# Rolling the rows of an 8192 x 8192 matrix by 100 columns: two rows in one flat copy of 65024 B instead of one row per copy

## The chip, the core and the metric

The kernel runs on one core of a Trainium2 chip. A core has compute engines (TensorE, VectorE, ScalarE, GpSimd), a SyncE that only issues work, and 16 DMA engines which move data between the chip's large memory (HBM, here called DRAM as well) and the on-chip memory SBUF, or from HBM to HBM. DMAs are issued by an instruction of SyncE (SP in the profile), ScalarE (ACT) or GpSimd (POOL). Each of the three has its own queue on every DMA engine. The metric is the device time of one execution in microseconds; lower is better.

## The reference

The kernel computes a roll along the columns: every element moves 100 columns to the right, and what leaves on the right comes back on the left of the same row.

```python
x = np.random.randn(8192, 8192).astype(np.float32)   # shift = 100
def reference(x, shift):
    return np.roll(x, shift, axis=1)     # out[r, c] = x[r, (c - 100) mod 8192]
```

Nothing is calculated. 256 MiB (268.44 MB) are read and as many written, and the work is in where the bytes go.

## The kernel before

In the code `s` is 100, `a` is 128 (the shift rounded up to 128 columns, so that a piece begins at a multiple of 512 B in the output) and `g` is 28. Each output row of 32768 B has two parts.

**The bulk**, columns 128 to 8191 (8064 elements, 32256 B), is one contiguous piece of the input row, at column 28. It is copied from DRAM to DRAM without touching SBUF. The rows are taken in 128 blocks of 64. Within a block, DMA `j` (0 to 3) takes the 16 rows `4e + j`, one for each DMA engine `e`; `j` = 0 and 2 are issued by SP, 1 and 3 by ACT (L41). So each DMA holds 16 pieces of 32256 B whose starts lie 128 KB apart. In the last four blocks a row is cut in two (15872 and 16384 B), two DMAs per `j`.

**The head**, columns 0 to 127 (512 B), consists of the row's last 100 input columns and its first 28. It goes through SBUF, on GpSimd's queue, in 16 stages of 512 rows (128 partitions x 4 rows). For rows 0 to 2 of a partition one DMA (L70) reads the 128 contiguous elements from the end of one input row across into the next row: 100 elements that belong to the head of row q, and 28 that belong to the head of row q + 1. Row 3's 100 elements (L71) and row 0's 28 (L74) come in two more DMAs straight into the tile `h`, and VectorE copies the rest from `t` to `h` (L72 and L75). Each stage has its own `t` and `h`. When all 16 stages have been asked for, 16 DMAs store the heads, 512 pieces of 512 B each (L78).

Heads and bulk write different columns, so no head waits for any bulk. The order of the work is that of the program on each queue: SP and ACT issue only bulk, GpSimd only heads, first 48 reads, then 16 stores. The framework that compiles the kernel gives 8 completion semaphores to the DMAs of SP and ACT together and 8 to those of GpSimd, and a DMA waits until the one that had its semaphore before has landed: each of SP and ACT has four DMAs in flight, GpSimd eight.

Of the kernel before, what the change touches and what calls it, by code (L numbers as in the profile page):

```python
# [1 line left out]

# [4 lines left out]


@with_exitstack
def kernel(  # L10
    ctx: ExitStack,
    tc: tile.TileContext,
    x: bass.AP,
    shift: int,
    out: bass.AP,
):
    nc = tc.nc
    n_rows, n_cols = x.shape
    s = shift % n_cols
    a = -(-s // 128) * 128  # L20
    g = a - s
    P = nc.NUM_PARTITIONS
    engines = [nc.sync, nc.scalar]
    n_chunks = 16
    rows = n_rows // n_chunks

    xm = x.rearrange("(c e j) w -> c j e w", e=16, j=4)
    om = out.rearrange("(c e j) w -> c j e w", e=16, j=4)
    if a < n_cols:
        blocks = n_rows // 64
        mid = (a + n_cols) // 256 * 128
        for c in range(blocks):
            parts = ((a, mid), (mid, n_cols)) if c >= blocks - 4 and a < mid else ((a, n_cols),)
            for j in range(4):
                for lo, hi in parts:  # L40
                    engines[j % 2].dma_start(out=om[c, j, :, lo:hi], in_=xm[c, j, :, lo - s:hi - s])  # L41
    if a == 0:
        return


    if a > 512:
        for i in range(n_chunks):
            r = slice(i * rows, (i + 1) * rows)
            nc.gpsimd.dma_start(out=out[r, :s], in_=x[r, n_cols - s:])
            if g > 0:  # L50
                nc.gpsimd.dma_start(out=out[r, s:a], in_=x[r, :g])
        return

    Q = 4
    n_st = n_rows // (P * Q)
    reads = ctx.enter_context(tc.tile_pool(name="reads", bufs=n_st))  # L60
    heads = ctx.enter_context(tc.tile_pool(name="heads", bufs=n_st))
    xt = x.rearrange("(k p q) c -> k p q c", q=Q, p=P)
    ot = out.rearrange("(k p q) c -> k p q c", q=Q, p=P)
    tiles = []
    for k in range(n_st):
        t = reads.tile([P, Q - 1, a], x.dtype)
        h = heads.tile([P, Q, a], x.dtype)
        lead = bass.AP(tensor=x.tensor, offset=(k * P * Q + 1) * n_cols - s,
                       ap=[[Q * n_cols, P], [n_cols, Q - 1], [1, a]])
        nc.gpsimd.dma_start(out=t[:], in_=lead, single_packet=True)  # L70
        nc.gpsimd.dma_start(out=h[:, Q - 1, :s], in_=xt[k, :, Q - 1, n_cols - s:], single_packet=True)  # L71
        nc.vector.tensor_copy(h[:, :Q - 1, :s], t[:, :, :s])  # L72
        if g > 0:
            nc.gpsimd.dma_start(out=h[:, 0, s:], in_=xt[k, :, 0, :g], single_packet=True)  # L74
            nc.vector.tensor_copy(h[:, 1:, s:], t[:, :, s:])  # L75
        tiles.append(h)
    for k, h in enumerate(tiles):
        nc.gpsimd.dma_start(out=ot[k, :, :, :a], in_=h[:], single_packet=True)  # L78


# [1 line left out]
_INS = ['x', 'shift']  # L82
_OUTS = [((8192, 8192), 'float32')]

_NUMBERS = {'shift': 100}


# [26 lines left out]
```

## Time and profile before

| what | value |
|---|---|
| time, median of 3 runs (lowest to highest) | 829.13 us (828.62 to 831.27) |
| span of the profiled execution | 818.3 us |
| the profiled execution's own time beside its span | not given by the page; the median is 10.8 us above the span |
| VectorE busy, GpSimd busy | 7.8 us, 41.1 us |
| bulk DMAs: SP and ACT | 248 whole-row and 16 half-row DMAs each |
| whole-row DMA, from issue to landing | 12.5 us (median) |
| head read (`t`), head store, from issue to landing | 32.6 us, 63.0 us (median) |

The page's parts are: busy times of the engines; the span in 40 slices (a digit is a busy share in tenths, DMA the mean share of the 16 DMA engines, GB/s what they moved, each byte counted once); the DMA queues (q1 and q10 are the two hardware queues of SP and ACT, q0 is GpSimd's), with their packets, megabytes and share of the 16 engines' time; the HBM traffic, in which a byte copied from HBM to HBM counts twice; and the issues with their time to landing. A bulk piece shows as one packet in the trace, and each DMA adds a 4 B packet per engine, which counts its semaphore up.

### The profile page before, as it was taken

Reading aid. Unit: us, or ns where it says so; the run is one execution under the profiler, and the core shown is the slowest. Engines: PE = TensorE matmul, PEld = TensorE weight load, DVE = VectorE, ACT = ScalarE, POOL = GpSimd, SP = SyncE. Lnnn points to the kernel's source line nnn. Section 1 sums busy time; section 2 is a strip of 40 time slices with the busy share of each in tenths; the row PEclk is TensorE's granted clock in tenths of the full one; section 3 lists DMA queues with packets and bytes.
Section 4 is the critical chain, followed back from the end, with each engine's and each line's share of the span. In section 5 each row is a group of like instructions: output and inputs, shape, how many; then the busy total and the mean of one; then the engine's idle time right before and its main releaser. Section 6 shows DMA issues by size and latency. Waiting matters only on the chain. (4 is left out here: it accounts for less than half of the span.)

```text
span 818.3 us, 689 instructions
## 1 busy us (share of the span) xinstructions
DVE 7.8 (1%) x32; POOL 41.1 (5%) x68
## 2 busy tenths in 40 slices
DVE  0000000000000000000000000000000000000000
POOL 3011111111010000000000000000000000000000
DMA  9999999999999999999999999999999999999998
GB/s 304 340 344 338 341 334 345 341 346 350 353 352 357 347 332 321 335 328 326 333 330 323 330 331 330 331 326 333 330 328 334 333 330 339 328 333 334 328 318 294
DMA packets 20229, 272.71 MB, mean 333 GB/s; under 512 B 9472, under 2 KB 9728, under 8 KB 11776
## 3 DMA queue, kind: packets, MB, share of 16 engines
q1 hardware_dynamic: 8448, 132.14, 48.2%
q10 hardware_dynamic: 8448, 132.14, 46.1%
q0 software_dynamic: 3328, 8.39, 4.7%
q14 instruction: 5, 0.04, 0.0%
HBM read 268.44 MB, written 268.44 MB: 656 GB/s over the span
## 5 line engine op out<-in xcount | busy, mean ns | idle before, releaser
L78 POOL DMA_DIRECT2D out_dram<-h x16 | 11.4, 712 | 87.2 <-DMA out_dram<-h 51.7
L70 POOL DMA_DIRECT2D t<-in_x_dram x16 | 12.1, 759 | 32.1 <-DMA h<-in_x_dram 31.3
L74 POOL DMA_DIRECT2D h<-in_x_dram x16 | 8.6, 538 | 85.7 <-DMA t<-in_x_dram 85.7
L71 POOL DMA_DIRECT2D h<-in_x_dram x16 | 8.9, 558 | 23.9 <-DMA h<-in_x_dram 23.9
L72 DVE COPY h<-t 128x300 f32<-128x300 f32 x16 | 5.9, 368 | 190.4 <-DMA t<-in_x_dram 190.4
L75 DVE COPY h<-t 128x84 f32<-128x84 f32 x16 | 3.2, 201 | 0.0
L95 POOL MEMSET const-float32-0.0<- 128x1 f32 x1 | 0.1, 99 | 0.2 <-issue 0.2
L95 POOL MEMSET const-bfloat16-1.0<- 128x1 bf16 x1 | 0.1, 101 | 0.0
L95 POOL MEMSET const-uint8-127<- 128x1 uint8 x1 | 0.1, 99 | 0.0
L95 POOL MEMSET const-float32-1.0<- 128x1 f32 x1 | 0.1, 98 | 0.0
## 6 DMA issues: line engine op xcount, KB each, us to landing
out_dram<-in_x_dram ACTq DMA_DIRECT2D x248, 504.0 KB, 12.5
out_dram<-in_x_dram SPq DMA_DIRECT2D x248, 504.0 KB, 12.5
out_dram<-h POOLq DMA_DIRECT2D x16, 256.0 KB, 63.0
t<-in_x_dram POOLq DMA_DIRECT2D x16, 192.0 KB, 32.6
out_dram<-in_x_dram SPq DMA_DIRECT2D x8, 256.0 KB, 5.9
out_dram<-in_x_dram ACTq DMA_DIRECT2D x8, 256.0 KB, 5.8
out_dram<-in_x_dram SPq DMA_DIRECT2D x8, 248.0 KB, 6.1
out_dram<-in_x_dram ACTq DMA_DIRECT2D x8, 248.0 KB, 6.1
```

Source lines behind the costliest of these rows:

```text
L70: nc.gpsimd.dma_start(out=t[:], in_=lead, single_packet=True)
L71: nc.gpsimd.dma_start(out=h[:, Q - 1, :s], in_=xt[k, :, Q - 1, n_cols - s:], single_packet=True)
L72: nc.vector.tensor_copy(h[:, :Q - 1, :s], t[:, :, :s])
L74: nc.gpsimd.dma_start(out=h[:, 0, s:], in_=xt[k, :, 0, :g], single_packet=True)
L75: nc.vector.tensor_copy(h[:, 1:, s:], t[:, :, s:])
L78: nc.gpsimd.dma_start(out=ot[k, :, :, :a], in_=h[:], single_packet=True)
L95: nc = _bacc.Bacc("TRN2", target_bir_lowering=False, num_devices=1)
```

## The change

For the first 15 of the 16 stages, rows are copied in pairs. One piece begins at column 128 of the first row and runs to the end of the second: 8064 + 8192 = 16256 elements, 65024 B, contiguous in the input and in the output. Per block of 64 rows SP issues one DMA (the pairs of rows `4e` and `4e + 1`) and ACT one (`4e + 2` and `4e + 3`), instead of two each.

Since the flat run is shifted by 100 elements across the row end, the first 100 columns of the second row receive the end of the row above, which is wrong there. They come right when the head of the second row is stored from SBUF, and so that store now has to follow the flat run. The framework sees that both write the same bytes: each head store of the stages 0 to 14 waits, on GpSimd, for the flat DMAs of its stage, on all eight semaphores of SP and ACT. The last stage (rows 7680 to 8191) keeps row pieces as before, halves in the last four blocks included; its heads wait for no bulk and are stored first. The head reads and VectorE's copies are the same, and their instructions still come first on GpSimd.

```diff
-    if a < n_cols:
-        blocks = n_rows // 64
-        mid = (a + n_cols) // 256 * 128
-        for c in range(blocks):
-            parts = ((a, mid), (mid, n_cols)) if c >= blocks - 4 and a < mid else ((a, n_cols),)
-            for j in range(4):
-                for lo, hi in parts:
-                    engines[j % 2].dma_start(out=om[c, j, :, lo:hi], in_=xm[c, j, :, lo - s:hi - s])
...
+    def piece(ring, row, lo, n):
+        o = row * n_cols + lo
+        dst = bass.AP(tensor=out.tensor, offset=o, ap=[[4 * n_cols, 16], [1, n]])
+        src = bass.AP(tensor=x.tensor, offset=o - s, ap=[[4 * n_cols, 16], [1, n]])
+        ring.dma_start(out=dst, in_=src)
...
-    for k, h in enumerate(tiles):
-        nc.gpsimd.dma_start(out=ot[k, :, :, :a], in_=h[:], single_packet=True)
+    per = G // 64
+    whole = n_st - 1
+    mid = (a + n_cols) // 256 * 128
+    tiles = [read_heads(k) for k in range(n_st)]
+    for c in range(n_rows // 64):
+        if c < whole * per:
+            for i, ring in enumerate(rings):
+                piece(ring, c * 64 + 2 * i, a, 2 * n_cols - a)
+        else:
+            parts = ((a, mid), (mid, n_cols)) if c >= n_rows // 64 - 4 and a < mid else ((a, n_cols),)
+            for j in range(4):
+                for lo, hi in parts:
+                    piece(rings[j % 2], c * 64 + j, lo, hi - lo)
+    nc.gpsimd.dma_start(out=ot[whole, :, :, :a], in_=tiles[whole][:], single_packet=True)
+    for k in range(whole):
+        nc.gpsimd.dma_start(out=ot[k, :, :, :a], in_=tiles[k][:], single_packet=True)
```

Here `rings` is SP and ACT, `G` is 512 (the rows of a stage) and `read_heads(k)` holds the head reads and copies of one stage as they were.

More of the change, by code (lines that the diff above doesn't have):

```diff
@@ L22, with read_heads @@
     P = nc.NUM_PARTITIONS
[L23 to L33, printed above, removed]
-    if a < n_cols:
-        blocks = n_rows // 64
-        mid = (a + n_cols) // 256 * 128
-        for c in range(blocks):
-            parts = ((a, mid), (mid, n_cols)) if c >= blocks - 4 and a < mid else ((a, n_cols),)
-            for j in range(4):
-                for lo, hi in parts:
[L41 to L51, printed above, removed]
+    rings = [nc.sync, nc.scalar]
+    if a == 0 or a > 512:
+        for i in range(16):
+            r = slice(i * n_rows // 16, (i + 1) * n_rows // 16)
+            rings[i % 2].dma_start(out=out[r, s:], in_=x[r, :n_cols - s])
+            if s > 0:
+                nc.gpsimd.dma_start(out=out[r, :s], in_=x[r, n_cols - s:])
         return
     Q = 4
-    n_st = n_rows // (P * Q)
+    G = P * Q
+    n_st = n_rows // G
+    xt = x.rearrange("(k p q) c -> k p q c", q=Q, p=P)
+    ot = out.rearrange("(k p q) c -> k p q c", q=Q, p=P)
+    def piece(ring, row, lo, n):
[3 more added lines that the diff above has]
+        ring.dma_start(out=dst, in_=src)
     reads = ctx.enter_context(tc.tile_pool(name="reads", bufs=n_st))
     heads = ctx.enter_context(tc.tile_pool(name="heads", bufs=n_st))
[L62 to L65, printed above, removed]
+    def read_heads(k):
         t = reads.tile([P, Q - 1, a], x.dtype)
         h = heads.tile([P, Q, a], x.dtype)
-        lead = bass.AP(tensor=x.tensor, offset=(k * P * Q + 1) * n_cols - s,
+        lead = bass.AP(tensor=x.tensor, offset=(k * G + 1) * n_cols - s,
                        ap=[[Q * n_cols, P], [n_cols, Q - 1], [1, a]])
@@ L75 @@
             nc.vector.tensor_copy(h[:, 1:, s:], t[:, :, s:])
-        tiles.append(h)
-    for k, h in enumerate(tiles):
-        nc.gpsimd.dma_start(out=ot[k, :, :, :a], in_=h[:], single_packet=True)
+        return h
+    per = G // 64
[14 more added lines that the diff above has]
+        nc.gpsimd.dma_start(out=ot[k, :, :, :a], in_=tiles[k][:], single_packet=True)
 _INS = ['x', 'shift']
```

## The prediction

> **What bounds the kernel now.** I read the page from the top: busy shares, the 40 slices, the queues, the DMA issues.
>
> ```profile
> span 818.3 us, 689 instructions
> DVE 7.8 (1%) x32; POOL 41.1 (5%) x68
> DMA  9999999999999999999999999999999999999998
> GB/s 304 340 344 338 341 334 345 341 346 350 353 352 357 347 332 321 335 328 326 333 330 323 330 331 330 331 326 333 330 328 334 333 330 339 328 333 334 328 318 294
> ...
> q1 hardware_dynamic: 8448, 132.14, 48.2%
> q10 hardware_dynamic: 8448, 132.14, 46.1%
> q0 software_dynamic: 3328, 8.39, 4.7%
> ...
> HBM read 268.44 MB, written 268.44 MB: 656 GB/s over the span
> ```
>
> No compute engine matters; the 16 DMA engines are busy from end to end (48.2 + 46.1 + 4.7 = 99.0% of their span). So the time is bytes over rate. Which rate? The stretches answer it (columns: stretch, length, DVE busy, POOL busy, clock, DMA share, GB/s).
>
> ```profile
> 15.00:200.00 185.00, 7.28 (x30) 28.15 (x45) 1.00 0.99 341
> 215.00:335.00 120.00, 0.00 (x0) 4.97 (x7) 1.00 1.01 343
> 345.00:500.00 155.00, 0.00 (x0) 0.00 (x0) 1.00 1.00 329
> 500.00:650.00 150.00, 0.00 (x0) 0.00 (x0) 1.00 0.99 330
> 650.00:790.00 140.00, 0.00 (x0) 0.00 (x0) 1.00 0.99 332
> 790.00:800.00 10.00, 0.00 (x0) 0.00 (x0) 1.00 0.88 310
> ```
>
> A row piece is read from HBM and written to HBM, a head only one of the two. Head reads (16 x 256 KB = 4.19 MB up to about 198 us) are 21 GB/s, head stores (4.19 MB from 174 to about 335 us) 26 GB/s. HBM traffic is then 2 x 341 - 21 = 661, 2 x 343 - 26 = 660 and 2 x 330 = 660 GB/s. Moved bytes differ by 4% between the stretches, HBM traffic does not. The packet records of the trace say the same from the engine's side: a 32256 B piece takes 1194 ns at best (27 GB/s for an engine, 432 for 16) but 1496 ns on average (1527 on q1, 1466 on q10), and between 345 and 790 us only 20 to 29% of the pieces run at that floor. The engines are busy because they wait on the memory.
>
> Then what feeds the engines, from the DMA issues and the waits:
>
> ```profile
> out_dram<-in_x_dram ACTq DMA_DIRECT2D x248, 504.0 KB, 12.5
> out_dram<-in_x_dram SPq DMA_DIRECT2D x248, 504.0 KB, 12.5
> out_dram<-h POOLq DMA_DIRECT2D x16, 256.0 KB, 63.0
> ```
> ```profile
> SPq L41 <- DMA out_dram<-in_x_dram: 671.1, 260, 4.8
> ```
>
> SP waits 671 us of 818 for landings: each ring holds four DMAs in flight (8 semaphores, half per ring; 4 x 818 / 264 = 12.4 us, the landing time shown), so issuing is hidden and an engine has pieces waiting. In the packet records the two rings alternate piece by piece on an engine (of 1683 pieces whose predecessor can be identified, 1673 follow one of the other ring).
>
> **The change, part by part.** The profile's own execution time is not given beside its 818.3 us span; the median of the three runs is 829.13, so 10.8 us lie around the span. I take the same 10.8 us for after.
>
> 1. *Bytes added.* 120 blocks x 2 rings x 16 engines = 3840 flat runs, each carrying 512 B of head that is stored again: 1.97 MB, read and written, 3.93 MB of HBM traffic on 536.87. At 656 GB/s that is +6.0 us; by DMA bytes (272.71 to 274.68 MB at 333 GB/s) +5.9. Nothing covers it, all engines being busy. I take +6.0. The Trainium skill (HBM Reference, Specifications) gives an HBM domain about 716 GB/s; by that figure the term would be 5.5 us, and this trace stays at 656, 92% of it.
>
> 2. *Pieces removed.* 7680 row pieces become 3840: 240 fewer per engine and 240 fewer 4 B semaphore writes (9 ns each in the records). What does a piece cost beyond its bytes? At the floor 16384 B take 611 ns and 15872 B 592, so 27 GB/s, and 9 ns are left over: 240 x 18 = 4.3 us. Under load the only other size is the half rows at the end: in 814 to 828 us on the trace's packet clock (which begins some 9 us before the span) they average 784 and 793 ns, 50 ns/KB, against 48 to 50 for whole rows; a few us earlier, with some engines idle, 43 to 47. Per piece that is between nothing and about 1.5 ns/KB x 15.75 KB = 24 ns above the whole rows, and since a piece's fixed cost shows half in that difference, at most some 50 ns: 0 to 12 us saved. Nearest to the mid-run state is the memory bound: an engine that saves 18 ns offers its next bytes sooner to a memory already full. I take a quarter of the 4.3 us: -1.0.
>
> 3. *Order of addresses.* On an engine rows 4e (SP), 4e+1 (ACT), 4e+2, 4e+3 become 4e and 4e+1 (SP), 4e+2 and 4e+3 (ACT). With strict alternation the engine walks the same addresses in nearly the same order, at the same 128 KB pitch between engines. Taken as 0; bounded by what the mid-run slices show of scatter, 318 to 339 around 330, or -2 to +4% (-20 to +30 us) if a pattern could hold one end; no such reason is seen.
>
> 4. *DMA size.* Four in flight per ring now mean 4 MB instead of 2, so an engine can run twice as far ahead of the slowest. In mid-run that can only fill idle time, at most the missing 0.5 to 1% of share, shown on engines that are memory bound: 0. At the step to smaller pieces it costs: the trace's 790 to 800 us, where whole rows give way to halves, has a share of 0.88, 1.2 us lost. The step from flat to row pieces (8 blocks before the end) is one more such step with pieces twice as long: 0 to 2.4 us, I take +0.5, since the slow engines speed up while the others idle.
>
> 5. *Heads, first part.* POOL's 48 head reads keep their order; each now takes turns with pieces of 65024 B. The reads' landings pace POOL (8 in flight), so the phase that ends at 198 us runs to about 390. VectorE's copies (368 + 201 ns a stage) are hidden: nobody needs them before the store.
>
> 6. *Heads, second part.* Store 15 goes first with no new wait. Each of the other 15 now waits on POOL for its stage's flat runs on all eight hardware semaphores; behind it queue only later stores. Between the stores of before lie 7 to 10 us, so I take 17. From 390 us they would need until 390 + 16 x 17 = 662, but a stage of bulk lands every 51 us; from about store 12 they follow the bulk. Stage 15's rows are 16.5 MB, 50 us of bulk, so stage 14's runs land at some 774 us (of 824), up to 787 with 12.5 us of spread; store 14 then takes 14 us (the shortest head landing in the trace) to 36 (the shortest store landing):
>
> ```profile
> DMA to landing us min/median/max: 14.4/33.4/65.3
> ```
>    It lands between 788 and 823, inside the end at 824. Cost 0; the cover is stage 15's bulk, and without it the last store would lie bare with 2 to 14 us.
>
> Removed issues (528 to 288) cost nothing: SP and ACT wait most of the time. Sum: 818.3 + 6.0 - 1.0 + 0.5 = 823.8 us of span, 834.6 us.
>
> **The rivals.** 0.3%, 2.5 us, is about what a measurement of this kernel can tell from no change.
>
> *Engine time, not memory, is the limit (same).* Then the added 512 B cost 512 / 32256 x 1496 = 24 ns a run, 240 x 24 = 5.7 us, and the two fixed costs saved, at 9 ns left over each, 4.3 us or a little more: +0 to +1.4, 829 to 830.5 us. For it: engines at 99%. Against it: the constant 660 GB/s.
>
> *A fixed cost per piece (faster).* If each piece pays 50 ns at its start (a stream that turns to another row), 240 of them are 12 us, less 6: 823 us. It decides from 25 ns a piece plus semaphore on. The extreme, that all the 302 ns above the floor belong to the piece, would give 240 x 302 = 72 us and 763 us; the half rows contradict it, since their excess over the floor is 154 ns (mean 755 over all four groups of halves, against 601), half of a whole row's. In this family falls a rule of the Trainium skill (DMA: Bandwidth & Descriptors, Measured): batch to 1 MiB or more for 75% of peak. It speaks for the change, 504 KB becoming 1016; with its fit of 2.0 us and bytes over 436 GB/s (Anatomy of one DMA), two of before would be 6.4 us and one of after 4.4, if done one by one. Here they are not: eight are in flight and the engines' share is 0.99, so what a fuller queue can fill is 1% of 818 us, 8 us, less 6: 827 us; 0.06 of this family's chance is on it.
>
> *The heads become the end (slower).* POOL's traffic now takes from some 15 to 335 us. If it gets 2.5 times slower instead of twice (15 + 2.5 x 320 = 815 us), several stores are left when the bulk is done; one that lands after the end costs 8 to 10 us at the pace of before, two or three +20: 855 us. For it: 63 us to land a store; against it: once the bulk thins out, POOL's 4096 B packets run at their floor of 159 ns.
>
> *Longer runs meet worse in memory (slower).* By the scatter above, +2%: 851 us. For it, only that nothing measures 64 KB pieces.
>
> **How the numbers follow.** My forecast 0.50 (its own range 831.6 to 842); engine time 0.13; fixed cost or better filling 0.22; heads at the end 0.06; worse in memory 0.09. Faster by over 0.3% comes to 0.23 with a little of the scatter, within 0.3% to 0.13, slower to 0.64. The range 819 to 848 leaves out about half of each slower rival and a third of the faster one.
>
> **What would show it.** Queues: q1 and q10 with 4608 packets each (120 x 16 + 24 x 16 = 2304 pieces and as many semaphores) and 133.1 MB. HBM still at 656 +/- 4 GB/s with 270.4 MB each way. Landing of the flat DMAs near 25 us. The last head read near 390 us, the last store issued near 780 and landed before the end. It is wrong if HBM traffic leaves 650 to 665 GB/s, if the chain ends in a head store, or if the flat runs come as several packets each.

## The result and the profile after

The changed kernel takes 840.75 us (median of 4 runs, 840.08 to 843.16), the kernel before on the same occasion 829.78: a ratio of 1.014, 95% interval 1.012 to 1.016. It is slower by 11 us. The forecast had the direction right and half of the size: +5.5 us, with 840.75 inside its range of 819 to 848. Each ratio with an interval, here and below, leaves out executions more than 1.5% above the fastest of their kernel; that concerns two of the six of the kernel with four rows per engine in one DMA, the profiled one among them, and five of the six of the kernel with rows 16 MB apart, which therefore has no ratio.

The page of after, with the lines that answer to those of before:

```profile
span 839.4 us, 495 instructions
...
DMA  9999999999999999999999999999999999999798
GB/s 314 336 331 332 332 327 325 326 335 333 323 332 325 324 334 327 331 340 322 339 333 327 350 332 342 329 318 346 327 339 315 346 325 335 328 328 326 257 304 295
...
q1 hardware_dynamic: 4608, 133.11, 46.9%
q10 hardware_dynamic: 4608, 133.11, 46.7%
...
HBM read 270.40 MB, written 270.40 MB: 644 GB/s over the span
...
out_dram<-in_x_dram ACTq DMA_DIRECT2D x120, 1016.0 KB, 26.0
out_dram<-in_x_dram SPq DMA_DIRECT2D x120, 1016.0 KB, 26.0
out_dram<-h POOLq DMA_DIRECT2D x16, 256.0 KB, 60.2
```

The bytes are as forecast (270.40 MB each way), a flat run is one packet (4608 packets per queue are 2304 pieces and their semaphores), and landing takes 26 us. HBM traffic over the span is 644 GB/s, below the 650 to 665 that the prediction set as its limits. What is new stands at the end of the two rows of slices: the 38th slice has a share of 7 tenths and 257 GB/s. In stretches (columns: stretch, length, DVE busy, POOL busy, clock, DMA share, GB/s):

```profile
500.00:650.00 150.00, 0.00 (x0) 2.14 (x3) 1.00 1.00 331
650.00:770.00 120.00, 0.00 (x0) 1.42 (x2) 1.00 1.00 331
...
779.00:789.00 10.00, 0.00 (x0) 0.00 (x0) 1.00 0.76 268
789.00:799.00 10.00, 0.00 (x0) 0.71 (x1) 1.00 0.82 296
799.00:809.00 10.00, 0.00 (x0) 0.00 (x0) 1.00 0.97 327
809.00:819.00 10.00, 0.00 (x0) 0.00 (x0) 1.00 0.77 234
819.00:829.00 10.00, 0.00 (x0) 0.00 (x0) 1.00 0.94 334
829.00:839.00 10.00, 0.00 (x0) 0.00 (x0) 1.00 0.80 268
```
```profile
779.00:839.00 60.00, 0.00 (x0) 0.71 (x1) 1.00 0.84 288
```

In the middle the engines are full. In the last 60 us they stand idle twice before the very end, near 780 to 799 us, where flat runs give way to row pieces, and near 809 to 819, where rows give way to halves.

One warning on the first comparison. After's profiled execution took 841.15 us with its span of 839.4, so 1.75 us lie around a span, not the 10.8 that the prediction took. The 818.3 us span of before thus belongs to an execution of about 820 us, quicker than the runs it was set beside. In the experiments below the same kernel before has medians from 818 to 829 us. Ratios are therefore always to the runs of before beside them, on the same chip, and the second profile of after and those of size without bytes and of bytes without size are compared with before's second one, taken beside them.

### The profile page after: what moved, and what is told of

It is laid out like the page before. It is cut to its first block, busy times and chain, and to the rows that moved or that the text cites. A ratio compares the mean times of both kernels' runs of the same rounds, so it can differ in the third digit from the quotient of the medians.

```text
span 839.4 us, 495 instructions
## 1 busy us (share of the span) xinstructions
DVE 7.8 (1%) x32; POOL 41.1 (5%) x68
## 3 DMA queue, kind: packets, MB, share of 16 engines
q1 hardware_dynamic: 4608, 133.11, 46.9%
q10 hardware_dynamic: 4608, 133.11, 46.7%
HBM read 270.40 MB, written 270.40 MB: 644 GB/s over the span
## 4 chain that ended last, share of the span: by engine, by line
DMA 94%; SPq 0%; issue 0%; POOLq 0%
DMA out_dram<-in_x_dram 94%; SPq L44 0%; POOLq L108 0%; POOLq L77 0%
```

## The experiments

Two causes were left for the 11 us: the 3.93 MB of extra HBM traffic, and something that the larger DMAs do at the end (*depth*: each ring's four DMAs hold twice the bytes, so an engine can run further ahead of the slowest, and later has to wait for it). Rivals were the longer piece itself and the head stores that wait.

### Before and after once more

Both kernels as they are.

> The kernel before, once more, for a second profile. After's profile has 1.75 us around its span (841.15 against 839.4), before's 818.3 us of span therefore stands for some 820 us, 9 us under its own median of 829.8. Theory 'the first profile was a quick execution': span near 828 us, HBM traffic in the middle (345 to 790 us) near 652 GB/s, as after has it (648 to 661). Theory 'longer pieces lower the memory's rate': span 818 to 822 us and 660 GB/s in the middle again. Time 829.8 us either way.

> The changed kernel beside the others on the same chip: 840.8 us. The share of the DMA engines falls below 0.9 in the last 45 us of span, as in its first profile (0.81, 0.88, 0.76 in 20 us steps from 784 us of span on).

Before 827.06 us (ratio to the shared runs of before 1.0004, 0.9987 to 1.0021), after 838.16 us (1.013, 1.0109 to 1.0152). Stretches of before's second profile:

```profile
500.00:650.00 150.00, 0.00 (x0) 0.00 (x0) 1.00 1.00 327
...
787.00:797.00 10.00, 0.00 (x0) 0.00 (x0) 1.00 1.01 331
797.00:807.00 10.00, 0.00 (x0) 0.00 (x0) 1.00 0.86 272
807.00:817.00 10.00, 0.00 (x0) 0.00 (x0) 1.00 0.98 339
817.00:827.00 10.00, 0.00 (x0) 0.00 (x0) 1.00 0.74 249
```
```profile
767.00:827.00 60.00, 0.00 (x0) 0.00 (x0) 1.00 0.93 306
```

And after's last 60 us in its second profile:

```profile
773.00:833.00 60.00, 0.00 (x0) 0.71 (x1) 1.00 0.88 297
```

Its span is 827.1 us and the middle has 2 x 327 = 654 GB/s of HBM traffic. After's first profile has 2 x 331 less its head stores' share there (three of 0.26 MB in 150 us, 5 GB/s) = 657, and its second, with 2 x 332 less the same 5, has 659. The memory is as fast under 65024 B pieces as under 32256 B ones; the 660 of the first profile was the quicker execution. Over the last 60 us, before has a share of 0.93 and after 0.88 here (0.84 in its first profile): 3 to 5 us more of idle engines. The share did not stay below 0.9 as expected: the dips of after's second profile (0.86 and 0.87) have a stretch of 0.98 between them.

### Size without bytes

```diff
+    def pair(ring, row):
+        o = row * n_cols + a
+        dst = bass.AP(tensor=out.tensor, offset=o, ap=[[4 * n_cols, 16], [n_cols, 2], [1, n_cols - a]])
+        src = bass.AP(tensor=x.tensor, offset=o - s, ap=[[4 * n_cols, 16], [n_cols, 2], [1, n_cols - a]])
+        ring.dma_start(out=dst, in_=src)
...
-                piece(ring, c * 64 + 2 * i, a, 2 * n_cols - a)
+                pair(ring, c * 64 + 2 * i)
```

> Two row pieces of 32256 B per engine in one DMA of 1008 KB, so the DMAs are as large and as few as after's, but no byte is stored twice, and no head store waits for bulk. Theory traffic (only the 3.93 MB count, 6 us): 829.8 us, as before. Theory depth (twice the bytes in flight per ring let the engines drift apart, and they idle when the pieces get smaller): 829.8 + 5 = 835 us, with the dip of the DMA share near 785 us. Theory long piece (a 65024 B piece is itself slower for the memory): 829.8 us, middle at before's rate.

The edit is to the changed kernel: one DMA takes two row pieces of 32256 B for each engine, and the heads between them are left out. 831.49 us, ratio 1.0058 (1.0037 to 1.0078): 4.8 us. The theory of depth had forecast 5. Its last 60 us:

```profile
772.00:782.00 10.00, 0.00 (x0) 0.00 (x0) 1.00 0.83 277
782.00:792.00 10.00, 0.00 (x0) 0.00 (x0) 1.00 0.81 245
792.00:802.00 10.00, 0.00 (x0) 0.00 (x0) 1.00 0.98 352
802.00:812.00 10.00, 0.00 (x0) 0.00 (x0) 1.00 0.76 235
812.00:822.00 10.00, 0.00 (x0) 0.00 (x0) 1.00 0.99 351
822.00:832.00 10.00, 0.00 (x0) 0.00 (x0) 1.00 0.77 259
```
```profile
772.00:832.00 60.00, 0.00 (x0) 0.00 (x0) 1.00 0.86 287
```

The same two dips as after, with pieces of before's length and no byte stored twice. 287 instead of 306 GB/s over 60 us are 1.14 MB, 3.5 us at 328 GB/s: most of the 4.8.

### Bytes without size

```diff
-                piece(ring, c * 64 + 2 * i, a, 2 * n_cols - a)
+                half = (2 * n_cols - a) // 2
+                piece(ring, c * 64 + 2 * i, a, half)
+                piece(ring, c * 64 + 2 * i, a + half, half)
```

> Each flat run of 65024 B cut into two DMAs with pieces of 32512 B: after's bytes and after's waits of the head stores, but before's number of DMAs, their size and bytes in flight. Theory traffic: 829.8 + 6 = 836 us if that is all of it, and then the other 5 us of after come from depth or from the long piece. Theory depth: 836 us, no dip near 785 us beyond before's (share 0.88 over 10 us). Theory 'the waiting head stores cost': 841 us, as after. Without any cost of bytes: 830 us.

832.9 us, ratio 1.0085 (1.0063 to 1.0107): 5.9 us of difference in the medians, 7.0 by the ratio. The end:

```profile
769.00:829.00 60.00, 0.00 (x0) 0.71 (x1) 1.00 0.95 319
```

No dip beyond before's (0.95 against 0.93). So this is the bytes' part, perhaps with the waits of the head stores. Half of its pieces begin, in the output, 256 B past a multiple of 512 B, which no piece of after does, and no run varies that alone; but after less size without bytes leaves about the same for the bytes, 0.7 to 0.8%. The two parts, 0.58 and 0.85%, add up to 1.43%; after has 1.3 to 1.4%. Within intervals of 0.2% each, nothing is left for the longer piece as such.

### Waits with almost no bytes

```diff
-            for i, ring in enumerate(rings):
-                piece(ring, c * 64 + 2 * i, a, 2 * n_cols - a)
+            for j in range(4):
+                piece(rings[j % 2], c * 64 + j, a, n_cols - a + (8 if j < 3 else 0))
```

> Row pieces and DMAs of before's size and number, but three of four pieces run 32 B over into the head of the next row in the first 15 stages, so that each head store has to wait for its stage's bulk as in the changed kernel, while only 0.18 MB are stored twice instead of 1.97. Theory traffic: 32 B cost 0.1%, 0.5 us, so the same as before within 0.3%, where the two-DMA version of the flat run had +0.85%. Theory 'what costs is that the head stores come late and wait': +0.6 to 0.9%, as with the full bytes. A third: a piece that ends in the middle of 64 or 512 B may cost something by itself, which would show as more than 0.3% with no dip at the end.

830.01 us against 829.2, ratio 1.0007 (0.9995 to 1.002): no change that can be told. The waits are there and long, as the lines of the head stores show:

```profile
L77 POOL DMA_DIRECT2D out_dram<-h x15: 709/709/756, 201.5 to 780.9; - x15
...
  DMA out_dram<-in_x_dram: 569.5, 13
...
DMA to landing us min/median/max: 13.5/14.2/35.6
```

GpSimd waits 569.5 us for bulk, and the last store goes out at 780.9 us and lands 14 us later, before the end at 829.1. So the waits cost at most 0.2%, and what the two-DMA version of the flat run paid was bytes.

### More depth, less depth, and no step

Four rows per engine in one DMA (`[n_cols, 2]` becomes `[n_cols, 4]`, the rings take blocks in turn); before with all rows in halves; and the pairs carried on to the last row. The first edit shown is to the kernel before, the second to the changed kernel with `pair` in the place of `piece`:

```diff
-            parts = ((a, mid), (mid, n_cols)) if c >= blocks - 4 and a < mid else ((a, n_cols),)
+            parts = ((a, mid), (mid, n_cols)) if a < mid else ((a, n_cols),)
```
```diff
-        if c < whole * per:
+        if c < n_rows // 64:
```

> Four row pieces per engine in one DMA of 2016 KB in the first 15 stages, the two rings taking blocks in turn: four times the bytes in flight of before, no byte stored twice. Before measured 827.0 us in the last session, the pairs 831.5 (+0.6%), and the pairs lost 4.2 us of DMA share in the last 60 us of span against before. Theory depth: the loss grows with the bytes in flight, 827 + 9 = 836 us, with the dips of the share in the last 80 us deeper and longer. Theory 'a step from one DMA size to another costs, however large': 831.5 us, as the pairs. Theory traffic alone: 827 us.

> The kernel before with every row cut into halves as in its last four blocks: half of before's bytes in flight per ring, twice the DMAs. Theory depth: the step at the end is gone and the engines stay closer together, up to 2 us less than before's 827 us. Against it, that four DMAs of 256 KB per ring are too little to keep the engines fed: share below 0.97 in the middle and 835 us or more. A fixed cost per piece and semaphore of 18 ns would add 528 / 16 x ... that is some 480 pieces per engine, 9 us: 836 us with the share at 1.00.

> The pairs DMA of 1008 KB for all 16 stages, so no step to smaller DMAs at all, and no byte stored twice. If the step itself makes the engines idle: 827 us, before's time. If the engines have drifted apart by then and the step only shows it: the idle time moves to the very end, 831 us or more, the last 10 to 20 us of the span at a share well under 0.8.

| bytes in flight per ring | ratio to before (95%) | DMA share, last 60 us | first to last engine of a DMA, us |
|---|---|---|---|
| halves, 1 MB | 1.0027 (1.0010 to 1.0044) | 0.98 | 1.7 |
| before, 2 MB | 1 | 0.93 | 6.0 (6.7 in its first profile) |
| pairs, 4 MB, with the small end | 1.0058 (1.0037 to 1.0078) | 0.86 | 18.7 |
| pairs to the end, 4 MB | 1.0130 (1.0109 to 1.0151) | 0.82 | 18.1 |
| four rows per engine (quads), 8 MB, with the small end | 1.0158 (1.0128 to 1.0188) | not compared | not compared |

Before's median beside these three was 818.32 us. From 2 MB in flight upward the price grows with depth, as that theory said. The lead itself stands in the last column: the trace records when each of the 16 engines counts a DMA's semaphore up, and the column has the median time from the first engine to the last, over the DMAs that land between 345 and 740 us (after has 15 us in both profiles). In the pairs kernel 12.8 of the 18.7 us lie between the last engine and the one before it: all the others lead one slow engine. Why one is slow stays open, and no run varied the number of DMAs in flight at one size, so bytes in flight and DMA size are not told apart. The step to smaller DMAs does not make the loss but shows it. Without the step it is larger and all in one place, at the end of the pairs carried through:

```profile
795.00:805.00 10.00, 0.00 (x0) 0.00 (x0) 1.00 1.02 342
805.00:815.00 10.00, 0.00 (x0) 0.00 (x0) 1.00 0.80 281
815.00:825.00 10.00, 0.00 (x0) 0.00 (x0) 1.00 0.11 48
```

In the last 10 us only a ninth of the engines' time is used, about two engines of 16, and the last eight DMAs still have 13 to 19 us between their first engine and their last. The row and half pieces of the last stage recover part of that: 1.3% without them, 0.6% with them. The halves keep the engines together, as the 1.7 us of the table and their last stretches show:

```profile
786.00:796.00 10.00, 0.00 (x0) 0.00 (x0) 1.00 0.99 322
796.00:806.00 10.00, 0.00 (x0) 0.00 (x0) 1.00 1.01 332
806.00:816.00 10.00, 0.00 (x0) 0.00 (x0) 1.00 0.89 304
```

But they are not faster over all (+0.27%). The fear that four small DMAs starve the engines did not come true (share 1.00 in the middle), nor did the 9 us of fixed cost; 2 us net, with some 3 us of idle end saved, leave about 5 us for 496 more pieces and semaphores per engine, some 10 ns each pair. That is one subtraction of small numbers and no more than a size.

### A finer end

```diff
+            cuts = 4 if c >= blocks - 4 else 2 if c >= blocks - 8 else 1
+            at = [a + (n_cols - a) // 128 * i // cuts * 128 for i in range(cuts)] + [n_cols]
+            parts = tuple(zip(at[:-1], at[1:]))
```

> The kernel before with a finer end: blocks 120 to 123 in halves, 124 to 127 in quarters (before: halves in the last four alone). Theory depth: engines are pulled together in two small steps instead of one; the loss of share at the end (4.4 us over the last 60 us in the second profile of before, the end's own edge included) goes down by some 1 us: 0.1% faster, hardly to be told from none. If small pieces cost by themselves: 0.1% slower.

825.5 us against 818.19, ratio 1.0092 (1.007 to 1.0113): neither theory. The end is starved:

```profile
792.00:802.00 10.00, 0.00 (x0) 0.00 (x0) 1.00 0.80 260
802.00:812.00 10.00, 0.00 (x0) 0.00 (x0) 1.00 0.83 262
812.00:822.00 10.00, 0.00 (x0) 0.00 (x0) 1.00 0.72 233
```
```profile
out_dram<-in_x_dram SPq DMA_DIRECT2D x24, 128.0 KB, 3.9
out_dram<-in_x_dram ACTq DMA_DIRECT2D x24, 128.0 KB, 3.9
```

A quarter piece of 8192 B takes 308 ns at best and 410 on average (packet records, q1), so eight of them, all that the two rings hold for an engine, last 2.5 to 3.3 us, and a DMA takes 3.9 us from issue to landing. The rings run dry before they are refilled. The reading fits the rows; no run varied it alone.

### Where the rows of a DMA lie

Three runs changed only which 16 rows form a DMA of before: neighbours (`"(c j e) w"`), every eighth (`j=8`), and one block of 512 rows for each engine (`"(e c j) w"`).

> The kernel before, but the 16 rows of a DMA lie next to each other (starts 32 KB apart instead of 128 KB), same pieces, same DMAs. It tests the step of the prediction that took the order of addresses as free. Nothing depends on addresses: 827 us and 653 GB/s in the middle. The memory serves some patterns better: another traffic in the middle, 820 to 850 us, in proportion.

> The kernel before with the 16 rows of a DMA 8 apart (256 KB) instead of 4 (128 KB). If more distance is better: up to 1% faster. If 128 KB was already enough: the same within 0.3%.

> The kernel before, but each DMA engine goes through its own 512 neighbouring rows, so the 16 pieces of a DMA start 16 MB apart instead of 128 KB; same pieces, same number of DMAs. Neighbouring rows (32 KB apart) gave +1.1% and 646 instead of 660 GB/s of HBM traffic in the middle. If more distance is better throughout: faster than before, by as much as 1%. If it is a matter of which distances collide in the memory: slower than before, by 1% or more.

| starts apart | ratio to before (95%), or time |
|---|---|
| 32 KB | 1.0109 (1.0061 to 1.0157) |
| 128 KB (before) | 1 |
| 256 KB | 1.0031 (1.0017 to 1.0045) |
| 16 MB | 1854.7 us (1481 to 2037) against 818.2 |

The six executions with neighbouring rows fall into two groups, 821 to 824 and 832 to 833 us, so the 1.1% is a mean of two. More distance, at 256 KB, did not make the kernel faster.

The prediction took the order of addresses as free because the change leaves it nearly as it was. That held; but order as such is not free. The page of the last one:

```profile
DMA  9999999999999999999999999999999999999999
GB/s 132 178 182 157 151 151 198 207 175 169 174 189 154 147 138 131 151 144 135 134 141 151 137 135 136 136 136 153 135 135 139 151 138 138 134 144 138 151 124 97
```

All engines count as busy, at 149 GB/s over the span: a full DMA row says nothing on whether the memory answers. The Trainium skill (DMA: Bandwidth & Descriptors, Latency and other measured facts) states that copies with a row pitch of large powers of two slow down, to 103 GB/s at 4 and 8 MiB from 207 at 512 KiB. The drop here at 16 MB agrees in kind. All distances tried here are powers of two, so whether it is the power of two or the distance that costs is not shown.

No version tried beats the kernel before.

## Why the prediction gave half of the change

*Step 1, bytes added, +6.0 us:* right. Measured 5.9 (medians) to 7.0 us (ratio), with the waits shown to cost no more than 0.2%. The reading behind it, that HBM traffic and not the engines sets the pace, holds: 654 GB/s before and 657 after in the middle. The 644 over the span crossed the prediction's own limit, and its reason is not a slower memory in the middle: the last 60 us move 288 GB/s instead of 331, and before's second execution has no more than 649 over its span either (536.87 MB in 827.1 us). The rival of longer runs that meet worse in memory falls with the middle's rate. The rival "engine time" would have given no more than +1.4 us, with the 4.8 of step 4 some 6 against the 11 measured, and falls too.

*Step 2, pieces removed, -1.0 us:* not seen by itself. The two parts sum to 1.43%, after has 1.3 to 1.4%, and the difference is smaller than the intervals. The rival of a fixed cost large enough to win falls, and better filling with it: the 1008 KB DMAs of size without bytes were 0.58% slower than before's 504 KB.

*Step 3, order of addresses, 0:* right for this change: the middle's rate did not move. The reason given, an order that hardly changes, was not tested by itself.

*Step 4, DMA size, +0.5 us:* this is the step that failed, by its size. It measured 0.58%, 4.8 us, twice the upper end that the step allowed (2.4). The mechanism was named (twice the lead over the slowest engine, paid at the step to smaller pieces), but sized at the 1.2 us idle of one step of before, at most doubled, and shaved because "the slow engines speed up while the others idle". They do, but only to 27 GB/s each (48 GB/s on 0.11 of 16 engines, last 10 us of the pairs to the end) from 21 (331 over 16). The runs showed a lead that went from 6 us to 15 and not just to twice, two dips instead of one, a price that more than doubles from 4 to 8 MB in flight, and a lead that must be paid at the end whether or not there is a step. The wider stretch of before would have warned: its last 60 us have a share of 0.93, which is 4 us, not 1.2.

*Steps 5 and 6, heads:* right in cost, 0. The reads took until about 426 us instead of 390 (store 15 waited 61 us for them), then eight stores (15 and 0 to 6) left within 7 us, not 17 us apart, since their bulk had long landed. So the stores caught up sooner than at store 12: from stage 9 on they went out at the pace of the bulk, some 51 us apart, the last at 792.8:

```profile
L77 POOL DMA_DIRECT2D out_dram<-h x15: 709/709/724, 427.3 to 792.8; - x15
...
  DMA out_dram<-in_x_dram: 355.2, 9
...
DMA to landing us min/median/max: 12.7/68.0/130.7
```

The last store takes the shortest time shown, 12.7 us, and lands at 805.5, 34 us before the end. The rival "the heads become the end" falls; the chain that ended last holds bulk copies for 94% of the span. The cover named for the last stores, stage 15's bulk, was there.

The sum had 5.5 us from 6.0 - 1.0 + 0.5; with the measured terms it is 6 to 7 + 5, against 11 measured. The 10.8 us "around the span" cancelled out of the difference, but the reading was wrong: 1.75 us lie there.

## What to carry over

When a copy is bound by memory traffic, as this one at some 655 GB/s, count each byte that is written twice at the full rate (here 6 to 7 us for 3.93 MB): the fewer and longer pieces that it buys were worth nothing that could be told, since the engines already wait for the memory. Larger DMAs, at four in flight per queue, let fast DMA engines run further ahead of a slow one (6 us at 504 KB, 19 at 1008 KB), and the lead is paid back at the end; price a larger DMA by the share of DMA time over the whole last stretch, not by one dip. Too little in flight seems to cost as well: where the work in flight (2.5 to 3.3 us) was shorter than a DMA's own time to land (3.9 us), the share fell to 0.72 to 0.83.

## What was not expected of the hardware

- Sixteen streams 16 MB apart ran at 149 GB/s instead of 333 over the span, with all DMA engines shown busy; 32 KB apart cost 1.1% and 256 KB 0.3% against 128 KB.
- The same kernel's median lay between 818 and 830 us from one set of runs to another (the experiments' four sets were on four chips), 1.4%, more than most effects studied here; only ratios to the runs of before beside them could be used.
- An ending cut into quarters (128 KB DMAs, 3.9 us to land) made the kernel 0.9% slower although it moved the same bytes in the same order.
